# Quads in strict product order, the attention branch opened with single quads, and a re-cut tail in a hybrid attention and state-space block

## Chip, cores and metric

The kernel runs on one core of one Trainium2 chip. The metric is the device time of one execution in microseconds (us); a median over runs is given. The core has five engines that work side by side, each on its own queue of instructions: TensorE (PE in the rows; PEld is its weight load), VectorE (DVE), ScalarE (ACT), GpSimd (POOL) and SyncE (SP, which issues most DMAs).

## What is computed

One layer on x of 256 rows and 2048 columns, all in fp32:

```python
proj = rms_norm(x, norm_w) @ w_in
q, k, v, z_a, z_s, xbc, dt_raw, g_a, g_s = split(proj)
o_a = mix(attention(q, k, v) for (window, dilation) in PATTERNS) * silu(z_a)
y   = rms_norm(ssd_scan(silu(conv(xbc)), dt, A) * silu(z_s), ssm_norm_w)
merged = sigmoid(g_a) * (o_a @ w_attn_branch) + sigmoid(g_s) * (y @ w_ssm_branch)
out = rms_norm(x + merged @ w_out, final_norm_w)
```

There are 16 attention heads of 128 columns and 64 state-space heads. The change touches the products with `w_ssm_branch`, with the columns of `w_in` for g_a and v, with `w_attn_branch` and with `w_out`, and what stands around them.

## The kernel before

**Stages.** The input projections with the state-space scan come first (0 to 575 us of the trace), then the ssm branch (to 754), g_a (to 834), v (to 915), the heads with q, k, z_a and attention (to 1207), the attention branch `attn` (to 1294), the output product `out` (to 1379), and a tail that normalises and stores.

**Precision.** Every fp32 operand is the sum of two rounded parts, h and l. A weight comes by DMA into the `w` ring; ScalarE copies it to `h` (L733), VectorE subtracts to `l` (L734). The rings of `h` and `l` have six slots, so a split writes where the split six before it stood and waits until TensorE has read that. One product of a 128x128 block of activations with 512 columns of weights is three matmuls into one PSUM bank: L771 (h and h), L772 (with the weights' l), L773 (with the activations' l).

**Quads.** `quads` (L760 on) makes a branch in two column halves (`cc` 0 and 1) of 1024 columns, eight quads each (sixteen in ssm). A quad is a 2x2 block product: rows of the two row halves i, two tiles of the inner dimension, two column blocks. In the plain form it takes eight products, in banks 2, 3, 4 and 8. A quad in `lefts` is a "seven": seven products from sums of blocks, into banks 1, 2, 3, 7, 5, 6, 4 in this order. It needs sums of the left operand (`left`, L677: four additions on VectorE, then a split of the first three sums, 128x768 for two quads, and one of the fourth, 128x256) and sums of the weights. For the quads in `STORED` these weight sums are made earlier, in the heads' stage (`store_sums`, L709), written to DRAM (`sums_d`) and loaded as `tq`. A quad's weights arrive as two pieces `wq` of 128x1024 (the first only 128x512 for a stored quad) and, if stored, two pieces `tq`; the splits are called `hq` and `lq`.

**What sets the order.** `in_turn("h", ...)` and `in_turn("l", ...)` keep the splits of quads in order on ScalarE and VectorE. Everything else is placed by the scheduler of the framework, which runs what it holds ready first; so TensorE's queue before may hold the L771 matmuls of several products ahead of the L772 of the first. Each engine works its queue off in the order that stands there. `then` is a table of functions that `quads` calls behind the n-th quad of its order: `turn_m` (L986) transposes 512 columns of the merged branch `th_s` in PSUM tiles `mtp` and splits them to `mT` (L243 on ScalarE, L245 on VectorE), `left_two` makes left sums, `fetch` loads x and the last norm's weights `fw`. PSUM banks come from three tags: "g" (four), "m1" and "m2" (two each).

**Tail.** `done` adds a bank's result to the residual row; ScalarE squares and sums it; `factor` makes the reciprocal root; `weigh` multiplies by `fw`; `put` scales and stores a piece.

## Time and profile before

| What | Value |
|---|---|
| Time, median of 3 runs | 1389.08 us (1388.73 to 1389.19) |
| Profiled execution | 1389.46 us, of which the span is 1387.7 us |
| Busy: PE, PEld, DVE, ACT | 1375.8, 1171.6, 1169.4, 832.6 us |
| Chain that ended last, by engine | PE 95%, DMA 2%, DVE 2%, ACT 1% |
| Mean granted clock of TensorE | 0.998 of full |
| DMA | 356.06 MB, 257 GB/s on the mean |

The profiled execution is one run with the hardware profiler; its span runs from the first to the last record, and 1.8 us of the time lie outside of it. The rows below come from this run. A row of the timeline gives the start in us from the span's start, the length, engine, line and operation with what is written and read, the count of instructions merged into it, and in brackets how long the engine had been idle before and who released it. A matmul of 512 columns is shown 0.39 us long, but the next starts 0.23 us after it, since matmuls overlap.

### The profile page before, as it was taken

How to read it: one execution, taken by the hardware profiler on the slowest of the kernel's cores; microseconds unless marked ns; L12 is line 12 of the kernel's file. 1: busy time of each engine (PE TensorE's matmuls, PEld its weight loads, DVE VectorE, ACT ScalarE, POOL GpSimd, SP SyncE). 2: the span in 40 equal slices, each digit the busy share in tenths (PEclk: the TensorE clock that was granted, in tenths of full speed). 3: DMA queues.
4: the chain of work that ended last, by engine and by line, in shares of the span. 5: the costliest groups of instructions: out<-in, count | busy, mean ns of one | idle time of the engine just before them, and what ended most of it. 6: DMA issues, size and time to landing. Idle time of an engine off the chain costs nothing.

```text
span 1387.7 us, 20440 instructions
## 1 busy us (share of the span) xinstructions
PE 1375.8 (99%) x7275; PEld 1171.6 (84%) x7275; DVE 1169.4 (84%) x1745; ACT 832.6 (60%) x1282; POOL 13.7 (1%) x66
## 2 busy tenths in 40 slices
...
DVE  6988889887898888699997888887787777677997
...
GB/s 336 211 216 289 257 299 273 255 326 272 286 260 278 236 245 183 180 183 243 170 236 204 295 290 266 282 327 301 297 298 288 282 293 225 159 234 291 301 205 189
DMA packets 102966, 356.06 MB, mean 257 GB/s; under 512 B 11536, under 2 KB 12240, under 8 KB 102224
## 3 DMA queue, kind: packets, MB, share of 16 engines
...
HBM read 322.14 MB, written 32.57 MB: 256 GB/s over the span
## 4 chain that ended last, share of the span: by engine, by line
PE 95%; DMA 2%; DVE 2%; ACT 1%; issue 0%; SPq 0%; DVEq 0%; ACTq 0%
PE ps_xs L303 8%; PE ps_zs L303 8%; PE ps_xs L306 4%; PE ps_zs L306 4%; PE ps_q L303 4%; PE ps_za L303 4%; PE ps_k L303 4%; PE ps_ssm L771 4%; PE ps_ssm L773 4%; PE ps_ssm L772 4%; PE ps_k L306 2%; PE ps_za L306 2%; PE ps_q L306 2%; PE ps_gs L369 2%; PE ps_gs L367 2%; PE ps_gs L368 2%
## 5 line engine op out<-in xcount | busy, mean ns | idle before, releaser
L236 ACT ACTIVATE h<-w 128x1024 fp32r<-128x1024 f32 (+1 forms) x293 | 306.1, 1047 | 278.2 <-PE ps_za L303 47.5
L237 DVE TENSOR_TENSOR l<-w,h 128x1024 fp32r<-128x1024 f32 (+1 forms) x293 | 352.9, 1207 | 105.0 <-ACT h L236 104.0
L734 DVE TENSOR_TENSOR lq<-wq,hq 128x512 fp32r<-128x512 f32 (+1 forms) x192 | 206.6, 1103 | 42.8 <-ACT hq L733 42.0
L733 ACT ACTIVATE hq<-wq 128x512 fp32r<-128x512 f32 (+1 forms) x192 | 179.2, 959 | 104.8 <-PE ps_attn L773 16.0
L303 PE MATMUL ps_xs<-XT,h 128*128 128x512 f32 x496 | 176.3, 396 | 0.0
L303 PE MATMUL ps_zs<-XT,h 128*128 128x512 f32 x496 | 175.4, 395 | 0.0
L306 PE MATMUL ps_xs<-XT,l 128*128 128x256 f32 x496 | 139.9, 282 | 0.0
L306 PE MATMUL ps_zs<-XT,l 128*128 128x256 f32 x496 | 139.4, 281 | 0.0
L303 PEld LDWEIGHTS ps_xs<-XT,h 128*128 128x128 f32 x496 | 93.2, 188 | 21.0
L303 PEld LDWEIGHTS ps_zs<-XT,h 128*128 128x128 f32 x496 | 93.1, 188 | 20.9
L306 PEld LDWEIGHTS ps_xs<-XT,l 128*128 128x128 f32 x496 | 93.7, 189 | 0.8 <-issue 0.3
L306 PEld LDWEIGHTS ps_zs<-XT,l 128*128 128x128 f32 x496 | 93.7, 189 | 0.3
L303 PE MATMUL ps_q<-XT,h 128*128 128x512 f32 x256 | 90.7, 393 | 0.0
L303 PE MATMUL ps_za<-XT,h 128*128 128x512 f32 x256 | 89.7, 392 | 0.0
L303 PE MATMUL ps_k<-XT,h 128*128 128x512 f32 x256 | 89.7, 392 | 0.0
L772 PE MATMUL ps_ssm<-lq,yT 128*128 128x512 f32 x216 | 83.9, 389 | 0.0
L773 PE MATMUL ps_ssm<-hq,yT 128*128 128x512 f32 x216 | 83.8, 389 | 0.0
L734 DVE TENSOR_TENSOR lq<-tq,hq 128x1024 fp32r<-128x1024 f32 x58 | 69.5, 1222 | 13.1 <-ACT hq L733 13.1
L733 ACT ACTIVATE hq<-tq 128x1024 fp32r<-128x1024 f32 x58 | 60.0, 1053 | 31.0 <-DMA tq<-sums_d 8.4
L771 PE MATMUL ps_ssm<-hq,yT 128*128 128x512 f32 x216 | 77.2, 390 | 0.0
L306 PE MATMUL ps_q<-XT,l 128*128 128x256 f32 x256 | 74.5, 291 | 0.0
L306 PE MATMUL ps_k<-XT,l 128*128 128x256 f32 x256 | 71.8, 280 | 0.0
...
## 6 DMA issues: line engine op xcount, KB each, us to landing
...
```

The source lines that it names most:

```text
L236: ac.activation(h[:, a:b], w[:, a:b], AF.Copy)
L237: last = ve.tensor_tensor(l[:, a:b], w[:, a:b], h[:, a:b].bitcast(F32), ALU.subtract)
L303: pe.matmul(acc[:width], h[:, kk, :], m, start=(kt == 0), stop=False)
L306: pe.matmul(acc[:width, S:], l[:, kk, :], m[:, :S], start=False, stop=(kt == n_kt - 1))
L367: pe.matmul(accs[i], xh, h, start=(kt == 0), stop=False)
L368: pe.matmul(accs[i], xh, l, start=False, stop=False)
L369: pe.matmul(accs[i], xl, h, start=False, stop=(kt == n_kt - 1))
L733: in_turn("h", ac.activation(h[:, cut:], src[:, cut:], AF.Copy))
L734: in_turn("l", ve.tensor_tensor(l[:, cut:], src[:, cut:], h[:, cut:].bitcast(F32), ALU.subtract))
L771: pe.matmul(accs[b], x[0], w[0], start=first, stop=False)
L772: pe.matmul(accs[b], x[0], w[1], start=False, stop=False)
L773: pe.matmul(accs[b], x[1], w[0], start=False, stop=stop)
```

## The change

1. `quads`: every product's first matmul is tied behind the last matmul of the product in front (`in_turn("pe", ...)`), so that TensorE's order is the program's. A plain quad goes row half by row half: banks 2 and 3, then 4 and 8.
2. `add_sums`: the loads of the weights for the heads' sums are tied behind the last split of the unit in front.
3. Attention branch, first half: the merged first pair of quads is gone; the calls stand in the heads' scope. The left sums for quads 1 and 3 are made ahead of the quads, in two pieces of 512; the last head's transposes and its mixing, with the left sums for quads 5 and 7, are called behind the first and second quads.
4. `STORED` for attn 1 gets quad 7 too, and its quads' order becomes (0, 2, 4, 1, 5, 3, 7, 6): all four odd quads take seven products. One more `store_sums` runs in the heads.
5. `fw` is loaded behind the sixth quad of out 0 instead of in `fetch`; the weightings of the first two column blocks go one quad later and behind the splits there.
6. Tail: row 0's piece 1536 to 2048 and the weighting of (1, 2) come behind the bank-8 addition; row 1 is cut to 320, 320, 512 on VectorE and 896 on ScalarE, and its last block is weighted and scaled in one operation (before: 320, 512, 512 on VectorE, 704 on ScalarE, the weighting apart).

```diff
-STORED = (("attn", 0, (3, 1, 5, 7)), ("attn", 1, (1, 3, 5)), ("out", 0, (5, 7)), ("out", 1, (1, 3, 7, 5)))
+STORED = (("attn", 0, (3, 1, 5, 7)), ("attn", 1, (1, 5, 3, 7)), ("out", 0, (5, 7)), ("out", 1, (1, 3, 7, 5)))
...
-    def add_sums(n, ts):
+    def add_sums(n, ts, tied=False):
         for j in range(2):
-            nc.sync.dma_start(ts[j], wq[n, :, j * UNIT : (j + 1) * UNIT])
+            fetch = nc.sync.dma_start(ts[j], wq[n, :, j * UNIT : (j + 1) * UNIT])
+            if tied:
+                paced(fetch)
...
-    def quads(tag, cc, x_of, n_kt, order, lefts, sums, finish, then={}, fold=None, first2=False, last2=False):
+    def quads(tag, cc, x_of, n_kt, order, lefts, sums, finish, then={}, fold=None, last2=False):
         accs = {}
         seven = [u for u in order if u in lefts]
         groups = [[u] for u in order]
-        if first2:
-            groups[:2] = [groups[0] + groups[1]]
         if last2:
...
-            pe.matmul(accs[b], x[0], w[0], start=first, stop=False)
+            in_turn("pe", pe.matmul(accs[b], x[0], w[0], start=first, stop=False))
             pe.matmul(accs[b], x[0], w[1], start=False, stop=False)
-            pe.matmul(accs[b], x[1], w[0], start=False, stop=stop)
+            behind["pe"] = pe.matmul(accs[b], x[1], w[0], start=False, stop=stop).ins.name
...
-                for b, i, c in ((2, 0, "1"), (3, 0, "2"), (4, 1, "1"), (8, 1, "2")):
+                for i, two in ((0, ((2, "1"), (3, "2"))), (1, ((4, "1"), (8, "2")))):
                     for v, w in zip(us, ws):
-                        product(b, block(2 * v, i), w["1" + c])
-                        product(b, block(2 * v + 1, i), w["2" + c], end and v == us[-1])
+                        for b, c in two:
+                            product(b, block(2 * v, i), w["1" + c])
+                            product(b, block(2 * v + 1, i), w["2" + c], end and v == us[-1])
...
-            after(S_LAG + 6, lambda a=(h, pT, za): mix(*a))
-            after(S_LAG + 3, lambda a=(h, p, pT): turn_p(*a))
+            if h < NH - 1:
+                after(S_LAG + 6, lambda a=(h, pT, za): mix(*a))
+                after(S_LAG + 3, lambda a=(h, p, pT): turn_p(*a))
...
+        def later(f):
+            tc.add_manual_dep(
+                f.ins, behind["l"], mybir.DependencyInfo(mybir.DependencyClass.NoSync, mybir.DependencyReason.DATA),
+                reason="behind the quads in front",
+            )
...
+        def left_two(src, sf, lefts, j0, two=scratch, step=2):
+            h4, l4 = sf[:, j0 : j0 + 2, 0], sf[:, j0 : j0 + 2, 1]
+            left(two, src, j0, 2, h4[:, :, :3], l4[:, :, :3], h4[:, :, 3], l4[:, :, 3], step=step)
+            for j in range(2):
+                lefts[2 * (j0 + j) + 1][:] = [(h4[:, j, e], l4[:, j, e]) for e in range(4)]
...
+        lefts = empty()
+        sf = mT[:, 8:16].rearrange("p k c -> p (k c)").rearrange("p (n a e s) -> p n a e s", n=4, a=2, e=4)
+        left_two(oaT, sf, lefts, 0, lambda: [vt[0][:, e * 512 : (e + 1) * 512] for e in range(2)], 1)
+        quads(
+            "attn", 0, lambda kt: oaT[:, kt, :], KT, (0, 2, 4, 3, 1, 5, 7, 6), lefts, lambda: four(spare), merged,
+            {0: lambda: turn_p(h, p, pT), 1: lambda: (mix(h, pT, za), left_two(oaT, sf, lefts, 2))},
+        )
...
             if c == 3 and i == 1:
-                put(0, 1024, 1536, ve, nc.sync)
-                put(0, 1536, 2048, ve, nc.sync)
-                in_turn("end", weigh(1, 2))
+                put(0, 1024, 1536, nc.sync)
                 in_turn("end", ve.tensor_tensor(row(i, c), fin[:, i, cs], a, ALU.add))
...
-                weigh(1, 3)
+                in_turn("end", weigh(1, 2))
+                put(0, 1536, 2048, nc.sync)
                 factor(1)
-                put(1, 0, 320, ve, nc.sync)
-                put(1, 1344, 2048, ac, nc.scalar)
-                put(1, 320, 832, ve, nc.sync)
-                put(1, 832, 1344, ve, nc.sync)
-
-        lefts = empty()
-        sf = mT[:, 8:16].rearrange("p k c -> p (k c)").rearrange("p (n a e s) -> p n a e s", n=4, a=2, e=4)
+                put(1, 0, 320, nc.sync)
+                put(1, 640, 1536, nc.scalar)
...
-            "attn", 0, lambda kt: oaT[:, kt, :], KT, (0, 2, 4, 3, 1, 5, 7, 6), lefts, lambda: four(spare), merged,
-            {0: lambda: (left_two(oaT, sf, lefts, 0), left_two(oaT, sf, lefts, 2))}, first2=True,
-        )
-        quads(
-            "attn", 1, lambda kt: oaT[:, kt, :], KT, (0, 2, 4, 1, 6, 3, 5, 7), {u: lefts[u] for u in (1, 3, 5)},
+            "attn", 1, lambda kt: oaT[:, kt, :], KT, (0, 2, 4, 1, 5, 3, 7, 6), lefts,
             lambda: four(spare), merged, {1: lambda: turn_m(0), 2: lambda: turn_m(1), 4: fetch},
...
-             6: lambda: left_two(mT, sf_m, lefts, 0)}, fold,
+             5: lambda: later(nc.sync.dma_start(fw, fw_d.partition_broadcast(P))), 6: lambda: left_two(mT, sf_m, lefts, 0)}, fold,
...
-            {n + 1: f for n, f in enumerate(weighted)}, fold, last2=True,
+            {n + 2: f for n, f in enumerate(weighted)}, fold, last2=True,
```

Where it moves instructions. The number behind `hq`, `lq`, `wq` and `tq` names the quad: 64 to 71 are quads 0 to 7 of attn 0, 72 to 79 those of attn 1. In brackets stand the engines or DMA queues that an instruction waits for.

**First place: the left sums of quads 5 and 7 of attn 0.** VectorE before: the additions and splits (L689 to L692, L695) of these sums stand among the splits of quads 67, 65 and 69.

```order
L690 SCALAR_TENSOR_TENSOR vt0_7717<-vt0_7717 128x2x128 [waits DVE_49]
L734 TENSOR_TENSOR lq65_11_12372<-wq65_0_12363,hq65_11_12371 128x512 [waits DMAHW0_49,Activation_49]
L734 TENSOR_TENSOR lq65_21_12376<-wq65_1_12365,hq65_21_12375 128x1024 [waits DMAHW1_49,Activation_49]
L734 TENSOR_TENSOR lq65_5_12380<-tq65_0_12367,hq65_5_12379 128x1024 [waits DMAHW2_49,Activation_49]
L692 TENSOR_TENSOR vt0_7717<-vt0_7717 128x2x128 [waits DVE_49]
L734 TENSOR_TENSOR lq65_4_12384<-tq65_1_12369,hq65_4_12383 128x1024 [waits DMAHW3_49,Activation_49]
L695 TENSOR_TENSOR mT_12183<-vt0_7717,mT_12183 128x2x384 [waits Activation_49]
L734 TENSOR_TENSOR lq69_11_12417<-wq69_0_12408,hq69_11_12416 128x512 [waits DMAHW4_49,Activation_49]
L734 TENSOR_TENSOR lq69_21_12421<-wq69_1_12410,hq69_21_12420 128x1024 [waits DMAHW5_49,Activation_49]
L734 TENSOR_TENSOR lq69_5_12425<-tq69_0_12412,hq69_5_12424 128x1024 [waits DMAHW6_49,Activation_49]
L695 TENSOR_TENSOR mT_12183<-vt0_7717,mT_12183 128x2x128 [waits Activation_49]
L734 TENSOR_TENSOR lq69_4_12429<-tq69_1_12414,hq69_4_12428 128x1024 [waits DMAHW7_49,Activation_49]
```

VectorE now (L687 to L694 are the sums, L736 the splits of weights, L697 those of the sums, which follow directly behind the last row):

```order
L687 TENSOR_TENSOR vt0_7717<-oaT_9149 128x1024 [waits DVE_49]
L736 TENSOR_TENSOR lq69_11_12427<-wq69_0_12418,hq69_11_12426 128x512 [waits DMAHW0_49,Activation_49]
L736 TENSOR_TENSOR lq69_21_12431<-wq69_1_12420,hq69_21_12430 128x1024 [waits DMAHW1_49,Activation_49]
L691 TENSOR_TENSOR vt0_7717<-vt0_7717 128x2x128 [waits DVE_49]
L693 TENSOR_TENSOR vt0_7717<-vt0_7717 128x2x128
L736 TENSOR_TENSOR lq69_5_12435<-tq69_0_12422,hq69_5_12434 128x1024 [waits DMAHW2_49,Activation_49]
L736 TENSOR_TENSOR lq69_4_12439<-tq69_1_12424,hq69_4_12438 128x1024 [waits DMAHW3_49,Activation_49]
L692 SCALAR_TENSOR_TENSOR vt0_7717<-vt0_7717 128x2x128 [waits DVE_49]
L736 TENSOR_TENSOR lq71_11_12472<-wq71_0_12463,hq71_11_12471 128x512 [waits DMAHW4_49,Activation_49]
L736 TENSOR_TENSOR lq71_21_12476<-wq71_1_12465,hq71_21_12475 128x1024 [waits DMAHW5_49,Activation_49]
L694 TENSOR_TENSOR vt0_7717<-vt0_7717 128x2x128 [waits DVE_49]
L736 TENSOR_TENSOR lq71_5_12480<-tq71_0_12467,hq71_5_12479 128x1024 [waits DMAHW6_49,Activation_49]
```

Before, the second L695 stands behind `lq69_5`; now the additions are spread over the splits of two quads and both L697 stand behind `lq71_5`.

ScalarE before, with the split of the same sums (L694, `mT`):

```order
L733 ACTIVATE hq65_5_12379<-tq65_0_12367 128x1024 [waits DMAHW2_49,DVE_49,PE_49]
L733 ACTIVATE hq65_4_12383<-tq65_1_12369 128x1024 [waits DMAHW3_49,DVE_49,PE_49]
L694 ACTIVATE mT_12183<-vt0_7717 128x2x384 [waits DVE_49]
L733 ACTIVATE hq69_11_12416<-wq69_0_12408 128x512 [waits DMAHW4_49,PE_49,Activation_49]
L733 ACTIVATE hq69_21_12420<-wq69_1_12410 128x1024 [waits DMAHW5_49,PE_49,Activation_49]
L733 ACTIVATE hq69_5_12424<-tq69_0_12412 128x1024 [waits DMAHW6_49,DVE_49,PE_49]
L694 ACTIVATE mT_12183<-vt0_7717 128x2x128 [waits DVE_49]
L733 ACTIVATE hq69_4_12428<-tq69_1_12414 128x1024 [waits DMAHW7_49,PE_49,Activation_49]
```

ScalarE now (L696, `mT`):

```order
L735 ACTIVATE hq69_5_12434<-tq69_0_12422 128x1024 [waits DMAHW2_49,PE_49]
L735 ACTIVATE hq69_4_12438<-tq69_1_12424 128x1024 [waits DMAHW3_49,PE_49]
L735 ACTIVATE hq71_11_12471<-wq71_0_12463 128x512 [waits DMAHW4_49,PE_49]
L735 ACTIVATE hq71_21_12475<-wq71_1_12465 128x1024 [waits DMAHW5_49,DVE_49,PE_49]
L735 ACTIVATE hq71_5_12479<-tq71_0_12467 128x1024 [waits DMAHW6_49,DVE_49,PE_49]
L696 ACTIVATE mT_12173<-vt0_7717 128x2x384 [waits DVE_49]
L696 ACTIVATE mT_12173<-vt0_7717 128x2x128 [waits DVE_49]
L735 ACTIVATE hq71_4_12483<-tq71_1_12469 128x1024 [waits DMAHW7_49,PE_49,Activation_49]
```

The split of the sums stood in front of and among the splits of quad 69; now it stands behind three splits of quad 71.

**Second place: attn 1 behind quad 4 (76).** TensorE before, from the end of quad 4 over the transposes (`mtp`) on:

```order
L773 MATMUL ps_attn1_8_12584<-hq76_11_12645,oaT_9149 128x512
L771 MATMUL ps_attn1_8_12584<-hq76_21_12649,oaT_9149 128x512
L772 MATMUL ps_attn1_8_12584<-lq76_21_12650,oaT_9149 128x512
L773 MATMUL ps_attn1_8_12584<-hq76_21_12649,oaT_9149 128x512
L994 MATMUL mtp10_12677<-ident2_9147,th_s_108 128x128 [waits DVE_49]
L994 MATMUL mtp00_12627<-ident2_9147,th_s_108 128x128 [waits DVE_49]
L994 MATMUL mtp00_12627<-ident2_9147,th_s_108 128x128 x2
L994 MATMUL mtp01_12634<-ident2_9147,th_s_108 128x128 x3
L994 MATMUL mtp10_12677<-ident2_9147,th_s_108 128x128 [waits DVE_49]
L994 MATMUL mtp10_12677<-ident2_9147,th_s_108 128x128 x2
L994 MATMUL mtp11_12684<-ident2_9147,th_s_108 128x128 x4
L771 MATMUL ps_attn1_2_12563<-hq73_21_12703,oaT_9149 128x512 [waits Activation_49]
```

TensorE now:

```order
L773 MATMUL ps_attn1_8_12604<-hq76_11_12665,oaT_9149 128x512
L771 MATMUL ps_attn1_8_12604<-hq76_21_12669,oaT_9149 128x512
L772 MATMUL ps_attn1_8_12604<-lq76_21_12670,oaT_9149 128x512
L773 MATMUL ps_attn1_8_12604<-hq76_21_12669,oaT_9149 128x512
L1020 MATMUL mtp10_12697<-ident2_9147,th_s_108 128x128
L1020 MATMUL mtp10_12697<-ident2_9147,th_s_108 128x128 [waits DVE_49]
L1020 MATMUL mtp10_12697<-ident2_9147,th_s_108 128x128 x2
L1020 MATMUL mtp11_12704<-ident2_9147,th_s_108 128x128 x4
L771 MATMUL ps_attn1_1_12735<-hq73_11_12719,oaT_9149 128x512 [waits DVE_49]
L772 MATMUL ps_attn1_1_12735<-lq73_11_12720,oaT_9149 128x512
L773 MATMUL ps_attn1_1_12735<-hq73_11_12719,oaT_9149 128x512
L771 MATMUL ps_attn1_2_12583<-hq73_21_12723,oaT_9149 128x512 [waits Activation_49]
```

Before, products of banks 2 and 3 follow the transposes and bank 1 comes some 30 rows later; now bank 1 follows at once and waits for VectorE.

**Third place: the tail.** VectorE before, from the bank-4 addition of row 1 on (L1030 is the reciprocal, L1037 and L1040 `put`, L1025 `weigh`, L1050 the bank-8 addition):

```order
L1052 TENSOR_TENSOR vt1_7718<-fin_12179,ps_out1_4_13329 128x512 [waits PE_49]
L1030 RECIPROCAL fs_12181<-fs_12181 128x1 [waits Activation_49]
L1037 SCALAR_TENSOR_TENSOR fin_12179<-vt1_7718,fs_12181,fw_12180 128x512 [waits DVE_49]
L1037 SCALAR_TENSOR_TENSOR fin_12179<-vt1_7718,fs_12181,fw_12180 128x512
L1025 TENSOR_TENSOR fin_12179<-vt1_7718,fw_12180 128x512
L1050 TENSOR_TENSOR vt1_7718<-fin_12179,ps_out1_8_13336 128x512 [waits PE_49]
L1025 TENSOR_TENSOR fin_12179<-vt1_7718,fw_12180 128x512 [waits DVE_49]
L1030 RECIPROCAL fs_12181<-fs_12181 128x1 [waits Activation_49]
L1040 TENSOR_SCALAR fin_12179<-fin_12179,fs_12181 128x320 [waits DVE_49]
```

VectorE now, from row 0's reciprocal on (L1040 the reciprocal, L1052 and L1049 `put`, L1035 `weigh`, L1061 the bank-8 addition):

```order
L1040 RECIPROCAL fs_12569<-fs_12569 128x1 [waits Activation_49]
L1052 SCALAR_TENSOR_TENSOR fin_12567<-vt1_7718,fs_12569,fw_12568 128x512 [waits DVE_49]
L1063 TENSOR_TENSOR vt1_7718<-fin_12567,ps_out1_4_13358 128x512 [waits PE_49]
L1061 TENSOR_TENSOR vt1_7718<-fin_12567,ps_out1_8_13365 128x512 [waits PE_49]
L1035 TENSOR_TENSOR fin_12567<-vt1_7718,fw_12568 128x512 [waits DVE_49]
L1052 SCALAR_TENSOR_TENSOR fin_12567<-vt1_7718,fs_12569,fw_12568 128x512
L1040 RECIPROCAL fs_12569<-fs_12569 128x1 [waits Activation_49]
L1049 TENSOR_SCALAR fin_12567<-fin_12567,fs_12569 128x320 [waits DVE_49]
L1049 TENSOR_SCALAR fin_12567<-fin_12567,fs_12569 128x320
```

The bank-8 addition had two `put` and a `weigh` in front of it; now one `weigh` and one `put` stand between it and row 1's reciprocal.

## Rows read from the trace of the kernel before

**Rows 1.** The page: busy line, VectorE's 40 slices, chain by engine.

```profile
PE 1375.8 (99%) x7275; PEld 1171.6 (84%) x7275; DVE 1169.4 (84%) x1745; ACT 832.6 (60%) x1282; POOL 13.7 (1%) x66
...
DVE  6988889887898888699997888887787777677997
...
PE 95%; DMA 2%; DVE 2%; ACT 1%; issue 0%; SPq 0%; DVEq 0%; ACTq 0%
```

**Rows 2.** Timeline of PE, 596 to 598 us: start us, us, engine, line, operation.

```profile
596.24 0.39 PE L773 MATMUL ps_ssm<-hq,yT 128*128 128x512 f32 x1
596.47 0.95 PE L832 MATMUL tot_y<-small,ssq 128*128 128x2 f32 x8
597.27 1.19 PE L771 MATMUL ps_ssm<-hq,yT 128*128 128x512 f32 x4
```

**Rows 3.** Timelines of DVE, then ACT, 1222 to 1235 us: lengths of splits and sums.

```profile
1223.78 1.82 DVE L734 TENSOR_TENSOR lq<-wq,hq 128x512 fp32r<-128x512 f32 x2
...
1225.85 0.42 DVE L691 TENSOR_TENSOR vt<-vt 128x256 f32<-128x256 f32 x1
1226.19 2.36 DVE L734 TENSOR_TENSOR lq<-tq,hq 128x1024 fp32r<-128x1024 f32 x2
...
1233.13 0.96 DVE L695 TENSOR_TENSOR mT<-vt,mT 128x768 fp32r<-128x768 f32 x1
...
1225.04 1.99 ACT L733 ACTIVATE hq<-tq 128x1024 fp32r<-128x1024 f32 x2
...
1230.31 0.83 ACT L694 ACTIVATE mT<-vt 128x768 fp32r<-128x768 f32 x1
```

**Rows 4.** Timeline of PE, opening of the attention branch.

```profile
1226.19 0.68 PE L771 MATMUL ps_attn<-hq,mT 128*128 128x512 f32 x2
1227.08 0.50 PE L771 MATMUL ps_attn<-hq,mT 128*128 128x512 f32 x1 [0.21 <-ACT hq L733]
...
1236.10 0.39 PE L773 MATMUL ps_attn<-hq,oaT 128*128 128x512 f32 x1
1236.62 0.50 PE L771 MATMUL ps_attn<-hq,mT 128*128 128x512 f32 x1
```

**Rows 5.** Timelines of PE, then DVE, at the end of the kernel.

```profile
1378.64 0.39 PE L773 MATMUL ps_out<-hq,mT 128*128 128x512 f32 x1
...
1379.98 0.68 DVE L1050 TENSOR_TENSOR vt<-fin,ps_out 128x512 f32<-128x512 f32 x1
...
1381.84 0.16 DVE L1030 RECIPROCAL fs<-fs 128x1 f32<-128x1 f32 x1 [0.45 <-ACT fs L1029]
1382.04 1.18 DVE L1040 TENSOR_SCALAR fin<-fin,fs 128x320 f32<-128x320 f32 x3
```

**Rows 6.** Timelines of DVE at 597 and 685 us, then PE at 685 us: ssm branch.

```profile
597.40 1.22 DVE L734 TENSOR_TENSOR lq<-wq,hq 128x1024 fp32r<-128x1024 f32 x1
...
684.76 4.11 DVE L734 TENSOR_TENSOR lq<-wq,hq 128x1024 fp32r<-128x1024 f32 x4
...
685.82 0.62 PE L771 MATMUL ps_ssm<-hq,yT 128*128 128x512 f32 x2
```

**Rows 7.** Timelines of PE, then DVE, 905 to 907 us: v.

```profile
905.03 0.39 PE L771 MATMUL ps_v<-hq,sf_x 128*128 128x512 f32 x1
906.18 0.51 PE L771 MATMUL ps_v<-hq,sf_x 128*128 128x512 f32 x1 [0.76 <-ACT hq L733]
...
906.15 1.23 DVE L734 TENSOR_TENSOR lq<-tq,hq 128x1024 fp32r<-128x1024 f32 x1 [3.69 <-ACT hq L733]
```

**Rows 8.** Timeline of PE, transposes; line L245: duration ns min/median/max.

```profile
1267.35 1.69 PE L994 MATMUL mtp<-ident,th_s 128*128 128x128 f32 x14
1268.80 0.48 PE L771 MATMUL ps_attn<-hq,oaT 128*128 128x512 f32 x1
...
L245 DVE TENSOR_TENSOR mT<-mtp,mT x8: 681/682/692, 1270.2 to 1315.0; 128x512 fp32r<-128x512 f32 x8
```

**Rows 9.** Windows: stretch, us, busy of PE, PEld, DVE, ACT, POOL, granted clock, DMA.

```profile
904.00:908.00 4.00, 3.24 (x15) 2.35 (x14) 1.84 (x2) 2.58 (x3) 0.00 (x0) 1.00 1.02 419
```

More of the change, by code (lines that the diff above doesn't have):

```diff
@@ L675, in hybrid_block, with left @@
         assert not trickle and not pieces
[L677 removed]
+    def left(two, src, j0, n, h3, l3, h4, l4, r=2, step=2):
         v = src.rearrange("p (n r) c -> p n r c", r=4)[:, j0 : j0 + n, r : r + 2, :]
[L679 to L680 removed]
+        for a in range(0, n, step):
+            m = min(step, n - a)
             js = slice(a, a + m)
             x, raw = two()
[L683 to L684 removed]
+            x = x[:, : 512 * m].rearrange("p (n k s) -> p n k s", n=m, k=2)
+            raw = raw[:, : 512 * m].rearrange("p (n e s) -> p n e s", n=m, e=4)
             ve.tensor_tensor(x, v[:, js, :, :S].bitcast(F32), v[:, js, :, S:].bitcast(F32), ALU.add)
@@ L964, in hybrid_block, with scratch, merged @@
         tick(final=True)
+        mT = big.tile([P, KT, 2 * S], F32R, name="mT", tag="xm")
+        spare = vt[0].rearrange("p (i c n) -> p i c n", i=2, c=2)
+        def scratch():
+            return [vt[0][:, e * UNIT : (e + 1) * UNIT] for e in range(2)]
+        def later(f):
[8 more added lines that the diff above has]
+                lefts[2 * (j0 + j) + 1][:] = [(h4[:, j, e], l4[:, j, e]) for e in range(4)]
+        wide.append(True)
+        empty = lambda: {u: [] for u in (1, 3, 5, 7)}
+        def merged(i, c, a, b, op):
+            cs = slice(c * 512, (c + 1) * 512)
+            ta, ts = th_a[i][:, cs], th_s[:, i, cs]
+            ve.tensor_tensor(b, a, b, op)
+            ve.scalar_tensor_tensor(ta, ta, 1.0, b, ALU.add, ALU.mult)
+            ve.scalar_tensor_tensor(ts, ta, 0.5, ts, ALU.mult, ALU.add)
+        lefts = empty()
[5 more added lines that the diff above has]
+        )
     with tc.tile_pool(name="fin", bufs=2) as fp:
@@ L970, in hybrid_block @@
         ac.activation(fs[:, 0, 15:16], ones2[:, 0:1], AF.Sqrt)
-        mT = big.tile([P, KT, 2 * S], F32R, name="mT", tag="xm")
-        spare = vt[0].rearrange("p (i c n) -> p i c n", i=2, c=2)
-        def scratch():
-            return [vt[0][:, e * UNIT : (e + 1) * UNIT] for e in range(2)]
         def fetch():
-            for f in (
-                nc.sync.dma_start(fin, x.rearrange("(i p) d -> p i d", p=P)),
-                nc.sync.dma_start(fw, fw_d.partition_broadcast(P)),
-            ):
-                tc.add_manual_dep(
-                    f.ins, behind["l"], mybir.DependencyInfo(mybir.DependencyClass.NoSync, mybir.DependencyReason.DATA),
-                    reason="behind the quads in front",
-                )
+            later(nc.sync.dma_start(fin, x.rearrange("(i p) d -> p i d", p=P)))
         def turn_m(c):
```

42 lines of the change are left out of this document (13 added, 29 removed).

## The prediction

> **What bounds the kernel now.** I read the page's busy line first, then the chain, then the engines' timelines where the diff works. TensorE is busy 99% of the span and holds 95% of the chain [rows 1]: the end is set by how many matmuls there are and by the few places where TensorE waits. VectorE is busy 84% on the mean, but its slices run from 6 to 9 tenths, so there are stages in which it is nearly full. Weights reach TensorE through splits: ScalarE writes the high part, VectorE the low part, both in rings of six slots, and a split can only start when TensorE has read the slot's former unit. The profiled execution took 1389.46 us, its span 1387.7; the median of the runs is 1389.08, 0.38 lower. I sum against 1389.46 and take the 0.38 off at the end. 0.2% is 2.8 us, about what a measurement of this kernel can tell from no change.
>
> **One product less.** Quad 7 of attn 1 becomes a seven: three matmuls fewer at 0.23 us, the distance of two neighbours [rows 2]: -0.69. Its sums are made in the heads' stage: four additions on VectorE of about 0.6 us (the 128x512 share of a pair of splits [rows 3]), two loads and two stores more. Slices 27 to 34, where the heads lie, show VectorE at 7 to 8 tenths [rows 1], so they are covered: 0. Without cover they would cost 2.4. The tie on the `st` loads only delays loads which nobody waits for: 0.
>
> **The opening of the attention branch.** Before, TensorE loses 0.44 us behind 1226.19 (two matmuls, so the next was due 1226.64, not 1227.08), 0.29 behind 1236.10 (0.52 to the next start, not 0.23), and 0.11 in each of the two matmuls that are shown 0.50 long instead of 0.39 [rows 4]. With single quads in front and the left sums for quads 1 and 3 made earlier these go: -0.95. They can also merely be replaced, which the waits below count.
>
> **The tail.** The last matmul ends at 1378.64 + 0.39 = 1379.03; the bank-8 addition starts 0.95 later, since VectorE has other work queued in front, and the reciprocal 1.86 after that [rows 5]. Now the addition comes first (0.05 after TensorE), but a weighting and a 128x512 store piece stand ahead of the reciprocal: three operations of 0.6 to 0.7, so it starts about 2.0 after TensorE instead of 2.81. The pieces behind it are about 0.3 us longer on VectorE, and a store of 256 KB is now among the last: -0.5, between -0.8 and +0.3. Moving `fw` and the other weightings is covered by a full TensorE: 0.
>
> **The strict order: five places where TensorE will now wait.** Before, the scheduler let TensorE run the h products ahead while a low part was still being made. The strict chain forbids that, so each product waits for its own l, with everything behind it.
> - *Third ssm quad.* l_21 starts at 597.40, takes 1.22 and is ready at 598.62 [rows 6]. TensorE is free at 597.27 (it ran four h products then [rows 2]); in strict order it wants l_21 four steps later, 598.19. Wait 0.4, with a hand-over 0.5. It is 0 if the split comes half a us earlier, 1.1 if it comes half a split later.
> - *ssm, second half.* Four splits back to back from 684.76 [rows 6]: the second is ready at 684.76 + 1.14 + 1.22 = 687.12; TensorE, whose next quad begins at 685.82, wants it four steps later, 686.74. Wait 0.4, with a hand-over 0.5 (0 to 1.2).
> - *v.* At 905.03 TensorE already loses 0.92 us waiting for a high part; now it waits for the low part, which starts at 906.15 and takes 1.23 [rows 7], so a matmul that started at 906.18 starts near 907.4. What it had run ahead is not lost, only later: +0.3 net (0 to 0.6).
> - *attn 0, quad 5.* Its product 3 reads the left sums of quads 5 and 7. In the new ScalarE queue `hq71_5` stands in front of their split, in VectorE's `lq71_5` (first place of the order). Say TensorE starts quad 3 at T. Quad 1's last h slot is read out after nine matmuls, T+2.1; its split takes 1.04 on ScalarE and 1.14 on VectorE, so the first sum starts near T+4.5. Between there and the last sum VectorE has one 1024-wide sum and four 1024-wide splits (1.14 each, the second of a pair), two 512-wide splits (1.82 - 1.22 = 0.60) and four small sums (0.34 from one start to the next): 8.3 us [rows 3]. It is done at T+12.8. Quad 5 starts 42 matmuls after T, near T+9.5, and wants product 3 six matmuls later, T+10.9. The high part is there 0.83 + 0.1 after the sum, T+13.7: wait 2.8. The low part must follow `lq71_5` (1.14) and takes 0.96: T+15.0, 0.7 to 0.8 after its matmul was due. Together 3.6. If VectorE were early, `hq71_5` alone, whose slot product 1 of quad 5 frees, would make it 2.1; with 0.2 for every hand-over it is 4.5. I take 3.6.
> - *attn 1, behind quad 4.* Bank 1 needs a PSUM slot that `mtp10` holds until VectorE has subtracted it (second place of the order). In ScalarE's and VectorE's queues the splits of `wq77` stand in front, and `hq77_21` waits for quad 4's last read. From there 0.95, 1.14, and 0.6 to 0.7 for the subtraction [rows 3, 8], with hand-overs and the first transposes' copies in front 3.0 to 3.6. TensorE has eight transposes meanwhile, 8/14 of the 1.45 that fourteen took, and some 0.2 for the change-over, about 1.0 [rows 8]. Before, products of other banks filled this. Wait 2.2 (1.9 to 2.6; 0 if the scheduler's own slot assignment frees another bank first).
>
> **Sum:** -0.69 - 0.95 - 0.5 + 0.5 + 0.5 + 0.3 + 3.6 + 2.2 = +5.0, so 1394.5 by the profiled execution's time and **1394.1** by the median. With every wait at its low bound but the last two at theirs (2.1 and 1.9) it is +1.9; with all high, the tail too, +8.7.
>
> **Rivals.**
> 1. *The strict order costs nothing.* Left sums and splits are there in time, because VectorE gets ahead in the plain quads 0, 2 and 4 that now open the branch; it decides from the point where the last sum of quads 5 and 7 is done 3 us earlier than I have it. Then the gains stand alone, -0.7 - 0.95 - 0.5 = -2.1, 1387.0; if the order also removes the 0.92 in v, 1386.1. For it: VectorE has slack in the tenths of most slices [rows 1]. Against: its queue is fixed, and the wanted sum stands behind six splits in it. 24%.
> 2. *Half of the waits.* Each wait gives both splitting engines time to fill their rings, so later ones shrink, or `mtp10` or the sums come a us or two earlier than I have them: 7.1/2 - 2.1 = +1.4, 1390.5. 22%.
> 3. *TensorE wins the waits back.* If it were not full, matmuls after a wait would come closer together until the lost time is made good, and the gains alone would be left: 1387.0. The rows speak against it: behind the 0.76 us of idle time at 906.18 [rows 7], as in the chain at 596 [rows 2], nothing is seen to start closer than 0.23 us. 2%. The Trainium skill ("Perfetto Trace Analysis", Identifying the Most-Contended Engine) holds that matmul busy time is no good measure of how near TensorE is to its limit and that LDWEIGHTS busy time is a better one; by that rule the 84% of PEld in the busy line would mean room for this rival.
> 4. *The clock falls behind the long wait.* The granted clock was 1.00 in the stretch that holds those 0.76 us [rows 9], its upper level of 2.4 GHz; no row shows a longer wait in the middle of matmuls. If the wait at quad 5 took it to 1.2 GHz for one seven, 21 steps of 0.23 would double: +4.8 on my sum, 1398.9. 6%. The Trainium skill ("TensorE: Matmul & The Clock Gate", Why this matters for your kernels) warns that idle gaps between bursts of matmuls can take the clock back to half; by that rule the wait is at risk, and no run here shows it yet.
>
> That the strict order might not be there is no rival: it stands in TensorE's queue as printed.
>
> **Chances and range.** My forecast has 46%; its own range is 1391.0 to 1397.8, by the bounds of the sum. Rival 1 splits by its two times: 14% faster by over 0.2% (below 1386.3), 10% within. Rival 2: 19% within, 3% slower. Rival 3: 2% within. The forecast: 1% within, 45% slower. Rival 4: 6% slower. So faster 14%, same 32%, slower 54%. Leaving out the lower part of rival 1 (10%), rival 4 and the top of the forecast, where all waits would be at their high bounds at once, the range is 1386.0 to 1397.0.
>
> **What would show it.** In the changed kernel's waits, TensorE's `ps_attn` should lead with two waits: one at product 3 of the third seven (on ScalarE's `mT` split, then VectorE's), 3 to 4 us together, and one behind the transposes after quad 4 (on VectorE's `mT`), about 2 us; small ones in `ps_ssm` near 598 and 687, on VectorE's l. The branch's opening should have none before the first seven, and the reciprocal of row 1 should start about 2 us after the last matmul. I am wrong if `ps_attn` waits under 1 us in all (rival 1), if the granted clock drops in any stretch (rival 4), or if TensorE's gaps lie elsewhere, in the out branch above all, where I count none.

## The result, and the profile after

The changed kernel takes 1396.01 us (median of 6 runs, 1394.63 to 1396.32); the kernel before, run on the same chips, 1389.12 (1388.55 to 1390.41). The ratio is 1.005, with a 95% interval of 1.004 to 1.006: slower by 6.9 us. Forecast were 1394.1, in a range of 1386.0 to 1397.0.

The page of the changed kernel, its lines for those of [rows 1]:

```profile
PE 1378.5 (99%) x7272; PEld 1171.9 (84%) x7272; DVE 1173.7 (84%) x1757; ACT 835.4 (60%) x1286; POOL 12.0 (1%) x66
...
PE 95%; DVE 3%; issue 1%; ACT 0%; DMA 0%; SPq 0%; DVEq 0%; ACTq 0%
```

The busy shares are those of before, to the per cent, and the shares of the chain differ by 2% at most: they don't show where 6.8 us of span came from. The waits of TensorE do (engine, line, waited for, us in total, times, longest):

```profile
PE ps_attn L771 <- ACT mT L696: 2.8, 1, 2.8
PE ps_attn L771 <- DVE mT L245: 2.1, 1, 2.1
PE warm L420 <- POOL ssq L417: 1.4, 1, 1.4
PE ps_first L329 <- ACT h L236: 0.8, 1, 0.8
PE ps_attn L773 <- DVE mT L697: 0.7, 1, 0.7
PE ps_ssm L772 <- DVE lq L736: 0.3, 2, 0.2
```

The two long waits that the prediction named lead the list, and the 0.7 on `mT` L697 is the low part behind the first. Those of `warm` and `ps_first` lie at the kernel's start and are there before too. But waits are not all. I cut both traces at the first matmul of each stage in TensorE's timeline, and the last at the end of the last matmul:

| us | start | ssm | g_a | v | heads | attn | out | tail | span |
|---|---|---|---|---|---|---|---|---|---|
| before | 585.45 | 168.39 | 80.24 | 81.34 | 291.31 | 87.33 | 84.97 | 8.66 | 1387.7 |
| changed | 585.24 | 170.11 | 80.24 | 80.24 | 291.31 | 94.45 | 85.10 | 7.83 | 1394.5 |
| difference | -0.2 | +1.7 | 0 | -1.1 | 0 | +7.1 | +0.1 | -0.8 | +6.8 |

**Quad 5 of attn 0.** TensorE's timeline there (start, length, engine, line, operation, and the idle time before with its releaser):

```profile
1236.08 0.39 PE L773 MATMUL ps_attn<-hq,oaT 128*128 128x512 f32 x1
1239.28 0.79 PE L771 MATMUL ps_attn<-hq,mT 128*128 128x512 f32 x1 [2.81 <-ACT mT L696]
1239.87 0.63 PE L772 MATMUL ps_attn<-lq,mT 128*128 128x512 f32 x1
1241.17 0.79 PE L773 MATMUL ps_attn<-hq,mT 128*128 128x512 f32 x1 [0.67 <-DVE mT L697]
1241.76 0.63 PE L771 MATMUL ps_attn<-hq,mT 128*128 128x512 f32 x1
...
1245.17 0.63 PE L773 MATMUL ps_attn<-hq,mT 128*128 128x512 f32 x1
1245.60 0.43 PE L771 MATMUL ps_attn<-hq,oaT 128*128 128x512 f32 x1
```

The same in windows (stretch, us, busy of PE, PEld, DVE, ACT and POOL with counts, granted clock, DMA share, GB/s):

```profile
1233.00:1236.00 3.00, 3.00 (x15) 2.49 (x14) 3.00 (x5) 2.45 (x4) 0.00 (x0) 1.00 0.94 341
1236.00:1239.20 3.20, 0.47 (x3) 0.04 (x1) 3.20 (x6) 2.27 (x4) 0.00 (x0) 0.95 1.02 362
1239.20:1242.40 3.20, 2.45 (x5) 1.54 (x6) 1.92 (x3) 0.38 (x2) 0.00 (x0) 0.50 0.90 312
1242.40:1245.60 3.20, 3.20 (x8) 2.43 (x8) 1.23 (x1) 1.70 (x2) 0.00 (x0) 0.50 0.85 334
1245.60:1248.80 3.20, 3.20 (x15) 2.66 (x14) 2.35 (x2) 2.29 (x4) 0.00 (x0) 0.99 0.62 206
```

Product 3 waits 2.81 us for the high part and its third matmul 0.67 for the low part. The twelve matmuls from 1239.28 on run at a granted clock of 0.50, the lower level of 1.2 GHz: from one start to the next 0.43 us, where it is 0.23 before the wait. The idle columns tell 3.5 us; from 1236.08 on the stretch to 1245.88 is 6.6 us longer than its 14 steps at 0.227 would be (9.80 less 3.18). The other 3.1 are the clock (2.6: nine steps 0.2 late, a tenth 0.05, and the two of 0.59 behind the waits 0.36 each) and what the waits take beyond the idle columns (0.5). This is one execution, with a mean granted clock of 0.996; the other five show 0.997 to 0.998, so the slow stretch need not be as long in each of them.

The two engines that TensorE waited for, ScalarE first:

```profile
1229.72 1.28 ACT L1008 ACT_TABLE_LOAD   x1
...
1237.06 0.83 ACT L696 ACTIVATE mT<-vt 128x768 fp32r<-128x768 f32 x1
1238.81 0.42 ACT L696 ACTIVATE mT<-vt 128x256 fp32r<-128x256 f32 x1 [0.93 <-DVE vt L694]
```

```profile
1238.37 0.41 DVE L694 TENSOR_TENSOR vt<-vt 128x256 f32<-128x256 f32 x1
1238.70 1.21 DVE L736 TENSOR_TENSOR lq<-tq,hq 128x1024 fp32r<-128x1024 f32 x1
1239.84 1.28 DVE L697 TENSOR_TENSOR mT<-vt,mT 128x768 fp32r<-128x768 f32 x2
```

It is the chain of the prediction: the last sum (L694) ends near 1238.8, its split on ScalarE follows at once, and on VectorE a weight split of quad 7 stands in front of the low parts (L697).

**Behind quad 4 of attn 1,** TensorE, then VectorE; it answers to [rows 8]:

```profile
1273.80 1.04 PE L1020 MATMUL mtp<-ident,th_s 128*128 128x128 f32 x8
1276.97 0.50 PE L771 MATMUL ps_attn<-hq,oaT 128*128 128x512 f32 x1 [2.13 <-DVE mT L245]
```

```profile
1275.09 1.22 DVE L736 TENSOR_TENSOR lq<-wq,hq 128x1024 fp32r<-128x1024 f32 x1 [0.28 <-ACT hq L735]
1276.24 1.28 DVE L245 TENSOR_TENSOR mT<-mtp,mT 128x512 fp32r<-128x512 f32 x2
```

Bank 1 waits 2.13 us until the first subtraction of `mtp10`, behind a split of 1.2 us, has read its slot.

**ssm,** at the place of [rows 6], TensorE:

```profile
685.75 0.39 PE L771 MATMUL ps_ssm<-hq,yT 128*128 128x512 f32 x1
686.31 0.50 PE L772 MATMUL ps_ssm<-lq,yT 128*128 128x512 f32 x1 [0.17 <-DVE lq L736]
```

The idle column says 0.17, but the start came 0.56 after the matmul in front, not 0.23: matmuls overlap, and a wait costs what the starts say. Such gaps at 597.9, 676, 685.8 and 686.9 and a slow step at 614.1, 0.1 to 0.45 each with the slow restarts behind them, sum to 1.6 us.

**Tail,** for [rows 5]; TensorE's last matmul ends at 1386.69:

```profile
1386.73 0.69 DVE L1061 TENSOR_TENSOR vt<-fin,ps_out 128x512 f32<-128x512 f32 x1 [0.67 <-PE ps_out L773]
...
1388.60 0.16 DVE L1040 RECIPROCAL fs<-fs 128x1 f32<-128x1 f32 x1
```

The bank-8 addition starts 0.04 after TensorE (before: 0.95), the reciprocal 1.91 after it (before: 2.81).

### The profile page after: what moved, and what is told of

It reads as the page before. It is cut to its first block, busy times and chain, and to the rows that moved or that the text cites. A ratio compares the mean times of both kernels' runs of the same rounds, so it can differ in the third digit from the quotient of the medians.

```text
span 1394.5 us, 20470 instructions
## 1 busy us (share of the span) xinstructions
PE 1378.5 (99%) x7272; PEld 1171.9 (84%) x7272; DVE 1173.7 (84%) x1757; ACT 835.4 (60%) x1286; POOL 12.0 (1%) x66
## 4 chain that ended last, share of the span: by engine, by line
PE 95%; DVE 3%; issue 1%; ACT 0%; DMA 0%; SPq 0%; DVEq 0%; ACTq 0%
PE ps_xs L305 8%; PE ps_zs L305 8%; PE ps_xs L308 4%; PE ps_zs L308 4%; PE ps_q L305 4%; PE ps_za L305 4%; PE ps_k L305 4%; PE ps_ssm L772 3%; PE ps_ssm L773 3%; PE ps_ssm L771 3%; PE ps_k L308 2%; PE ps_za L308 2%; PE ps_q L308 2%; PE ps_gs L370 2%; PE ps_gs L371 2%; PE ps_gs L369 2%
## 5 line engine op out<-in xcount | busy, mean ns | idle before, releaser
L736 DVE TENSOR_TENSOR lq<-wq,hq 128x512 fp32r<-128x512 f32 (+1 forms) x192 | 206.5, 1098 | 48.6 <-ACT hq L735 47.8
L736 DVE TENSOR_TENSOR lq<-tq,hq 128x1024 fp32r<-128x1024 f32 x60 | 71.5, 1219 | 15.6 <-ACT hq L735 15.5
L771 PE MATMUL ps_ssm<-hq,yT 128*128 128x512 f32 x216 | 84.3, 390 | 0.0
L773 PE MATMUL ps_ssm<-hq,yT 128*128 128x512 f32 x216 | 84.1, 389 | 0.0
L735 ACT ACTIVATE hq<-tq 128x1024 fp32r<-128x1024 f32 x60 | 62.3, 1053 | 35.1 <-PE ps_attn L773 12.8
```

The costliest lines, as they stand in the source:

```text
L735: in_turn("h", ac.activation(h[:, cut:], src[:, cut:], AF.Copy))
L736: in_turn("l", ve.tensor_tensor(l[:, cut:], src[:, cut:], h[:, cut:].bitcast(F32), ALU.subtract))
L771: in_turn("pe", pe.matmul(accs[b], x[0], w[0], start=first, stop=False))
L773: behind["pe"] = pe.matmul(accs[b], x[1], w[0], start=False, stop=stop).ins.name
```

## The experiments

All edits are against the changed kernel, unless said otherwise. Of each profiled execution the stages as above:

| us | ssm | v | attn | out | tail | span |
|---|---|---|---|---|---|---|
| before | 168.39 | 81.34 | 87.33 | 84.97 | 8.66 | 1387.7 |
| changed | 170.11 | 80.24 | 94.45 | 85.10 | 7.83 | 1394.5 |
| e1_free | 168.39 | 80.24 | 84.61 | 86.76 | 10.32 | 1387.7 |
| e2_chain | 170.28 | 80.95 | 89.85 | 85.28 | 7.74 | 1391.4 |
| e3_order | 170.20 | 80.24 | 88.20 | 85.11 | 7.85 | 1388.3 |
| e4_fill | 170.25 | 80.44 | 94.30 | 85.11 | 7.84 | 1394.6 |
| e5_swap | 170.16 | 80.24 | 93.08 | 85.12 | 7.84 | 1394.1 |
| e7_best | 168.42 | 80.23 | 86.74 | 85.13 | 7.83 | 1384.8 |
| e8_parts | 168.37 | 80.24 | 86.70 | 85.38 | 7.84 | 1385.7 |
| e9_real | 170.17 | 80.24 | 93.94 | 85.10 | 7.84 | 1396.2 |
| e10_all | 168.41 | 80.24 | 85.76 | 85.13 | 7.84 | 1384.7 |
| e11_three | 168.39 | 81.16 | 87.66 | 85.74 | 7.74 | 1387.5 |
| e12_zeros | 170.07 | 80.24 | 92.63 | 85.10 | 7.84 | 1392.9 |

g_a (80.2) and the heads (291.3) are the same in all. The start (585 to 587) varies with waits for the first weights that are in every kernel, and in e9_real also with 3.4 us at a granted clock of 0.50 behind such a wait; so stages are compared, not single spans.

**e1_free: the strict order taken out.**

```diff
-            in_turn("pe", pe.matmul(accs[b], x[0], w[0], start=first, stop=False))
+            pe.matmul(accs[b], x[0], w[0], start=first, stop=False)
...
-            behind["pe"] = pe.matmul(accs[b], x[1], w[0], start=False, stop=stop).ins.name
+            pe.matmul(accs[b], x[1], w[0], start=False, stop=stop)
```

> The changed kernel without the strict order: the tie between products is dropped, everything else stays. My theory: the tie itself makes the waits, 2.8 + 0.7 us at product 3 of quad 5, 2.1 behind quad 4 of attn 1 and 1.7 in ssm, and the slow matmuls behind the first of them (2.6 us) come with it; without it TensorE runs other products there, and only v's 0.9 comes back: 1396.0 - 8.0 to -9.5 + 0.9, near 1387 to 1389. Rival: the waits come from ScalarE's and VectorE's queues, in which the left sums stand late whatever TensorE does; then ssm alone gains and the time is 1393 to 1395.

Measured: 1389.42 us, 1.0005 of the kernel before (0.9995 to 1.0015). All waits in attn above 0.25 us are gone and ssm is back at 168.39, though the left sums of quads 5 and 7 have the same place in the program: the strict order makes the waits. It does so in two ways at quad 5. The first is that TensorE may not run other products ahead. The second is that the scheduler places the sums later: here the last sum, on VectorE, and its split, on ScalarE, stand at

```profile
1235.45 0.42 DVE L694 TENSOR_TENSOR vt<-vt 128x256 f32<-128x256 f32 x1
1236.26 0.40 ACT L696 ACTIVATE mT<-vt 128x256 fp32r<-128x256 f32 x1
```

so the sum ends 29.9 us after the start of attn (1205.99); in the changed kernel it ends 31.6 after it (1207.14). Product 3 was due there 29.2 after it, so of its 2.8 us some 1.5 would be left with these sums in the strict order; that is an estimate, no run has this pair. Two things I had not expected. v keeps its 80.24, so v's gain does not come from the order; the row halves of the plain quads are the only other part of the change that stands in v. And the tail grows to 10.32. VectorE there:

```profile
1376.04 1.88 DVE L1063 TENSOR_TENSOR vt<-fin,ps_out 128x512 f32<-128x512 f32 x3 [2.16 <-PE ps_out L773]
1378.92 0.16 DVE L1040 RECIPROCAL fs<-fs 128x1 f32<-128x1 f32 x1 [1.00 <-ACT fs L1039]
...
1379.79 0.68 DVE L1061 TENSOR_TENSOR vt<-fin,ps_out 128x512 f32<-128x512 f32 x1
```

The banks of the last pair of quads end close together, three additions run back to back, and bank 8's starts at 1379.79, 2.4 us after TensorE's last matmul (1376.97 + 0.39).

**e2_chain: the kernel before with the strict order alone** (the reverse of the diff above, on the kernel before).

> The kernel before with the strict order alone: each product tied behind the one in front, nothing else of the change. My theory: ssm becomes 1.7 us longer and v 1.1 shorter as in the changed kernel, and the attention branch, whose left sums for four sevens are made between splits, waits for them by 3 us or more, with slow matmuls behind a long wait: 1392 to 1397. Rival: the strict order costs only in ssm, and the waits in attn come from the new places of the left sums and the new order of quads: 1389.5 to 1390.5.

Measured: 1393.49 us, 1.0038 (1.0023 to 1.0053). ssm takes 170.28, and attn 2.5 us more than before. But the wait is not where I had it: the left sums cost under 0.3, and bank 1 behind quad 4 costs 2.6. So the long wait at quad 5 needs the order and the late sums, the one behind quad 4 the order alone. And the old tail code gets 7.74. The wait, then VectorE at the end:

```profile
PE ps_attn L771 <- DVE mT L245: 2.6, 1, 2.6
```

```profile
1383.65 0.69 DVE L1050 TENSOR_TENSOR vt<-fin,ps_out 128x512 f32<-128x512 f32 x1 [0.76 <-PE ps_out L773]
...
1385.52 0.17 DVE L1030 RECIPROCAL fs<-fs 128x1 f32<-128x1 f32 x1 [0.45 <-ACT fs L1029]
```

The addition starts 0.03 after TensorE with the old order of store pieces.

**e3_order: a plain quad between sevens 3 and 1.**

```diff
-            "attn", 0, lambda kt: oaT[:, kt, :], KT, (0, 2, 4, 3, 1, 5, 7, 6), lefts, lambda: four(spare), merged,
+            "attn", 0, lambda kt: oaT[:, kt, :], KT, (0, 2, 3, 4, 1, 5, 7, 6), lefts, lambda: four(spare), merged,
```

> The changed kernel with attn 0 in the order (0, 2, 3, 4, 1, 5, 7, 6) instead of (0, 2, 4, 3, 1, 5, 7, 6): plain quad 4 stands between sevens 3 and 1. The left sums of quads 5 and 7 and their split then stand ahead of quad 5's own splits on both engines. My theory: both waits at quad 5 go (3.5 us) and so do the slow matmuls behind them (2.6): 1396.0 - 6 = 1390, granted clock 1.00 all through; the 2.1 us behind quad 4 of attn 1 stays. Rival: the clock falls there for another reason than the wait: 1392.5, with 2.6 us of matmuls at half clock left.

Measured: 1391.28 us, 1.0016 (1.0006 to 1.0025); the profiled execution 1390.07, one of the shortest of ten. In it attn is 6.25 shorter (the medians differ by 4.7), and of the waits in attn one is left, the untouched one:

```profile
PE ps_attn L771 <- DVE mT L245: 2.1, 1, 2.1
...
PE ps_ssm L772 <- DVE lq L736: 0.4, 2, 0.2
```

No matmul runs at 0.43 us steps in this execution. With the wait at quad 5, the slow stretch behind it goes.

**e4_fill, e9_real and e12_zeros: the wait filled with matmuls.** Is it the idling that lowers the clock?

```diff
+    ac.activation(zero, ssq[:, 0, :P], AF.Copy)
...
+                if tag == "attn" and cc == 0 and u == 5:
+                    for _ in range(12):
+                        behind["pe"] = pe.matmul(accs[2], zero, w["21"][0], start=False, stop=False).ins.name
                 product(3, s4, w["22"], end)
```

> The changed kernel with twelve matmuls of a zero block (they add zero to bank 2) between products 2 and 3 of quad 5, 12 x 0.227 = 2.7 us, where TensorE waits 2.8 us now. The left sums come as late as before. My theory: the clock falls because TensorE idles; with the wait filled product 3 starts at the same time, no matmul runs at half clock, and 2.6 us are won: 1393.4. Rival: the clock falls for another reason, or the shorter wait of 0.7 us behind it is enough: the matmuls of quad 5 stay at 0.43 us steps and the time at 1396.

Measured: 1395.07 us, 1.0046 (1.0031 to 1.0061): 0.9 below the changed kernel, with an interval that holds the changed kernel's 1.005, and not the 2.6 that I had expected. Twelve were too few: waits of 0.38 and 1.16 us were left, and behind them

```profile
1236.00:1239.20 3.20, 3.20 (x15) 2.44 (x13) 3.20 (x6) 2.07 (x3) 0.00 (x0) 1.00 0.96 353
1239.20:1242.40 3.20, 1.66 (x6) 0.96 (x6) 2.39 (x4) 0.58 (x2) 0.00 (x0) 1.00 0.89 298
1242.40:1245.60 3.20, 3.20 (x9) 2.50 (x9) 1.45 (x2) 1.95 (x2) 0.00 (x0) 0.54 0.92 362
```

the clock fell all the same, for eight matmuls. That left two readings: the idle rest, or the zeros. e9_real puts seventeen matmuls there that read the blocks of product 2 (twelve from the lines above with these operands, five more tied to product 3, which the scheduler placed at the same spot):

> The changed kernel with seventeen matmuls of real data (3.9 us) in the wait at quad 5, where e4_fill had twelve of a zero block; they add a repeated product to bank 2, which is not in the reference. In e4_fill eight matmuls behind the wait still ran at half clock. My theory: it was the idle rest (0.4 + 1.2 us), or the zeros; with real data and no rest every matmul of quad 5 follows in 0.23 us, granted clock 1.00, and the attention branch is some 2.5 us shorter than the changed kernel's 94.4. Rival: the fall has another cause than idling: half clock again behind 1239.

Measured in its one profile: a wait of 0.40 left for the low part, no matmul of quad 5 at 0.43, and

```profile
1239.20:1242.40 3.20, 3.20 (x16) 2.65 (x15) 3.20 (x5) 1.32 (x3) 0.00 (x0) 1.00 0.98 339
1242.40:1245.60 3.20, 2.80 (x13) 2.00 (x12) 1.47 (x3) 1.30 (x2) 0.00 (x0) 1.00 1.00 389
```

but attn was only 0.5 shorter, not 2.5, since the seventeen take longer (3.9 us) than the wait that they fill (3.0) and here the clock fell behind the other wait, that of 2.13 us in attn 1: 0.61 in this stretch, seven steps at 0.43:

```profile
1276.80:1280.00 3.20, 2.90 (x8) 2.30 (x9) 1.31 (x3) 1.06 (x1) 0.00 (x0) 0.61 0.55 190
```

e12_zeros, seventeen of zeros in the loop above, tells the two readings apart:

> The changed kernel with seventeen matmuls of a zero block in the wait at quad 5: as e9_real in number and place, with zeros for data. e4_fill (twelve of zeros) kept waits of 0.4 and 1.2 us and fell to half clock, e9_real (seventeen of real data) did not. My theory: the idle rest in e4_fill was the cause; with seventeen the granted clock stays at 1.00 behind quad 5, as with real data. Rival: matmuls of zeros don't keep the clock up; behind 1240 the steps are 0.43 us again.

Measured in one profile: 1.00 throughout, with a wait of 0.68 left for the low part; attn is 92.63, 1.8 shorter than in the changed kernel, although seventeen matmuls (3.9 us) now take the place of a wait of 3.0.

```profile
1239.20:1242.40 3.20, 2.52 (x11) 1.80 (x10) 2.38 (x4) 0.59 (x2) 0.00 (x0) 1.00 0.77 282
1242.40:1245.60 3.20, 3.20 (x15) 2.63 (x14) 2.12 (x2) 2.58 (x3) 0.00 (x0) 1.00 0.92 371
```

So at quad 5 the clock fell in the three profiles that had more than 1.5 us of idle time left there (the changed kernel, e4_fill, and e5_swap below) and in neither of the two whose fill left 0.7 or less: the idle time is the cause that these runs point to, with one profile for each kernel, and zeros held the clock as real data did.

**e5_swap: other PSUM tags for the transposes.**

```diff
-                tag = (("m2", "m1"), ("g", "g"))[c % 2][pair]
+                tag = (("g", "g"), ("m2", "m1"))[c % 2][pair]
```

> The changed kernel with the transposes' PSUM tags exchanged: the first pair (mtp00, mtp01) takes slots of tag g, the second (mtp10, mtp11) of m2 and m1. Bank 1 of quad 5 in attn 1 then needs a slot that VectorE frees two subtractions earlier. My theory: the 2.1 us behind quad 4 go, and bank 7, nine matmuls later, waits 0 to 0.7 for the second pair: attn 1.5 to 2.1 us shorter than 94.4. Rival: VectorE is late as a whole there (splits of quad 77 in front), so the wait only moves to bank 7: less than 0.7 won.

Measured in one profile: the 2.1 become 0.7, at bank 7, and attn is 1.4 shorter. The wait was for the PSUM slot, and two thirds of it could be moved out of the way:

```profile
PE ps_attn L771 <- DVE mT L245: 0.7, 1, 0.7
```

**e7_best, e8_parts, e10_all: keeping what gains.** e7_best joins e3_order, e5_swap and `if tag != "ssm":` in front of the tie. e8_parts keeps the tie in g_a, v and out alone; e10_all is that with e3_order's line:

```diff
-            in_turn("pe", pe.matmul(accs[b], x[0], w[0], start=first, stop=False))
+            lead = pe.matmul(accs[b], x[0], w[0], start=first, stop=False)
+            if tag not in ("ssm", "attn"):
+                in_turn("pe", lead)
```

> The changed kernel with the order of attn 0 as in e3_order, the exchanged tags of e5_swap, and the strict order dropped in ssm alone. My theory: the parts add up, ssm 168.4, v 80.2, attn 88.2 - 1.9 = 86.3, out and tail as in the changed kernel: 1386.5, that is 2.5 below the kernel before. Rival: the freed queue moves waits elsewhere, above all in attn, where VectorE stays as full as it was: 1388 to 1390.

> The changed kernel with the strict order kept in ga, v and out and dropped in ssm and attn. My theory: the strict order is worth having where it lets results leave early (tail 7.8 instead of 10.3 in e1_free) and in v (80.2 instead of 81.3), and costs in ssm and attn: ssm 168.4, v 80.2, attn and out together near 170.5, tail 7.9: 1386 to 1387. Rival: the long tail of e1_free comes from attn running late into out, not from the order in out: tail above 9.5, 1388 to 1389.

> The changed kernel with the strict order kept in ga, v and out, dropped in ssm and attn (as e8_parts), and with attn 0 in the order of e3_order. My theory: the left sums are there in time and TensorE may run other products ahead behind the transposes, so attn loses neither the 0.8 us of e7_best nor the 0.8 of e8_parts at quads' changes: attn and out together near 171.1, 1386.5, 2.3 below the kernel before. Rival: nothing is left to win there, 1387.3 as the two others.

Measured: e7_best 1387.32 us, 0.9988 (0.9979 to 0.9996); e8_parts 1387.38, 0.9991 (0.9982 to 1.0000); e10_all **1386.39 us, 0.9984 (0.9975 to 0.9993)**: by the ratio some 2.2 us below the kernel before (by the medians 3.0: 1389.35 on the same chip), faster, though by less than the 0.2% that I had set. e7_best missed by 0.8 us, with the 0.7 of e5_swap at bank 7 left; e8_parts missed too: attn and out take 172.1 together, not 170.5. e8_parts' tail is 7.84, so the long tail of e1_free came from the lack of the order in out. In e10_all's waits of TensorE no branch is left:

```profile
PE warm L420 <- POOL ssq L417: 1.4, 1, 1.4
PE ps_first L329 <- ACT h L236: 1.2, 2, 0.9
```

**e11_three: the kernel before with the tie in g_a, v and out** (the last diff, on the kernel before, with the line of e1_free's diff that marks each product's last matmul).

> The kernel before with the strict order in ga, v and out alone; its old tail, old attn and old order of ssm stay. My theory: the gain in v (1.1, less the 0.7 that e2_chain lost there) and the shorter tail (7.8 instead of 8.7) come from the strict order, not from the new pieces of the tail: 1389.0 - 0.4 - 0.9 = 1387.6, last matmul to end 7.8. Rival: the tail's gain needs the new order of store pieces: tail 8.6, 1388.4.

Measured: 1389.30 us, 1.0003 (0.9995 to 1.0012). The tail is 7.74, with the old pieces: as my theory had it. v won only 0.2, attn lost 0.3, and out lost 0.8, most of it in one wait for VectorE's fold of a bank (0.5 at 1342), so the time stands still; my 1387.6 missed for that.

## Why the prediction was right

The waits that the strict order makes came where the prediction has them and decide the result. That the time lies inside the range is in part luck: against the sum of +5.0 the clock added 2.6, ssm 0.7 and the waits at quad 5 0.4 (4.0 from start to start), while v fell short by 1.4 and the tail by 0.3.

- **One product less** (-0.69) is in every count of matmuls and was not measured apart; the heads stayed at 291.31, so the extra sums and the tied loads cost nothing, as said.
- **The opening** (-0.95): its gaps of [rows 4] are gone, and between 1207.6 and 1236 no matmul of 512 columns now starts more than 0.1 us late behind the one in front.
- **The wait at quad 5** (3.6): 2.81 + 0.67 = 3.48. The mechanism was right (a late sum in the queues, and a TensorE that may not go on without it), its parts less so: counted from quad 3's start (1224.75) the last sum ended at T+14.0, not T+12.8, among other things behind a table load of 1.28 us on ScalarE that I had not counted; the product was due at T+11.6, not T+10.9, since head 15's products lie in quad 3; and the split it waits for is the small one, 0.42, not 0.83. The errors cancelled: that 3.6 came so near is luck.
- **The wait behind quad 4** (2.2): 2.13; e5_swap shows the slot as its cause.
- **ssm** (+1.0): mis-sized. The two places were right, with 0.3 at the first and two gaps of together 0.9 at the second, and there are more, at 614 and 676: +1.72, and 168.4 again in each kernel without the order there.
- **v** (+0.3): wrong. In the changed kernel the order costs nothing there; -1.1. I assumed that the wait for the high part would stay and the low part come on top. The wait of 0.92 in [rows 7] goes, with the strict order or without (e1_free), once plain quads go row half by row half; with the order and the old quads v took 80.95 and 81.16 (e2_chain, e11_three).
- **The tail** (-0.5): -0.83, but for another reason than the step gives. The old pieces with the strict order give 7.74 in both profiles (e2_chain, e11_three), the new ones 7.83, and the new ones without it 10.32. The strict order ends the banks one after another, so that row 0 is finished before bank 8 is; the re-cut by itself won nothing that shows.
- **The clock**: I had it as a rival that excludes the forecast, at 6%, and named a drop of the granted clock as a sign of being wrong. That sign came, and it came with the forecast. Twelve slow matmuls, some 2.6 us by their steps, are more than the 1.9 that the sum of +5.0 lacks to +6.9; the rival's own price, 4.8, was too high. The Trainium skill ("TensorE: Matmul & The Clock Gate", Why this matters for your kernels) warns that idle gaps between bursts of matmuls can cost half the clock, and the trace agrees: granted clock 0.50 behind 2.81 us of idle TensorE.
- **Waits are not won back**: behind none of them do matmuls of 512 columns start closer together than 0.22 us, as close as two stand in the kernel before. The Trainium skill's rule on LDWEIGHTS busy time ("Perfetto Trace Analysis", Identifying the Most-Contended Engine) would have seen 16% of room; that share reads 84% in both kernels, 6.9 us apart, and told nothing about either.
